# A hybrid decoder trunk on one core: the recurrent branch's gate tiles computed in a fifth product stage

## The chip, the cores and the metric

One core of a Trainium2 chip runs the whole program. The metric is the device time in microseconds (us) of one execution. TensorE (PE) multiplies, VectorE (DVE), ScalarE (ACT) and GpSimd (POOL) work elementwise, SyncE (SP) only issues transfers. Each engine takes its instructions in the order of the program and waits for the others through semaphores. A transfer is issued by SP or POOL, in that queue's own order too.

## The reference

One layer over 1024 tokens of width 1024, all float32. The normalised, modulated input `h` goes through one projection, whose column groups feed two branches; the branches are gated, merged and projected back.

```python
h = rms_norm(x, norm_w[l]) * (1.0 + scale[:, None, :]) + shift[:, None, :]
proj = h @ w_in[l]
hq, hf, hi, hz, gq, gk, gv, gz, ga, mg = jnp.split(proj, IN_OFFSETS, axis=-1)
y_h = hgrn2_branch(hq, hf, hi, hz, lb_all[l], hgrn_norm_w[l])     # ... return rms_norm(o, norm_w) * silu(hz)
y_g = gla_branch(gq, gk, gv, gz, ga, ...)                         # ... return rms_norm(o, norm_w) * silu(gz)
u_h = y_h @ w_branch[l, 0]
u_g = y_g @ w_branch[l, 1]
mg = jax.nn.sigmoid(mg.reshape(B, T, N_BRANCH, D_MODEL))
merged = mg[:, :, 0] * u_h + mg[:, :, 1] * u_g
x = x + gate[:, None, :] * (merged @ w_out[l])
return rms_norm(x, final_norm_w)
```

Both branches are chunked linear attention with a decay for each key channel (8 heads of 128 in the recurrent branch `hgrn2`, 4 heads in `gla`). The change is about `silu(hz)`: 1024 columns of the projection, the gate of the recurrent branch.

## The kernel before

Every float32 matrix product is done as three fp32r products: each operand is split into a rounded part `hi` (a cast on ACT) and a rest `lo = x - hi` (a subtraction on DVE), and `hi*hi + hi*lo + lo*hi` is accumulated. All large tiles are slots of 128 x 1024 float32; there are 46 (`N_SLOTS`), handed out first in, first out, so a slot that was just freed is taken last.

The program has three parts.

**The stream** (`Stream.go`). A list of jobs runs one after the other on PE. A `Feat` job computes 128 columns of the projection for all 1024 tokens: 8 steps of 6 matmuls 128x512 (L455). For each recurrent head there are three, for `hq`, `hf` and `hz`. `Vblk` and `Vblk2` (L514 to L516, L557 to L559) do the values. Each job's weights are loaded up to two jobs ahead and split one job ahead. After each step of 6 matmuls `weave` lets two other tracks put in work: the side track (`attention` of the heads that are ready, faster by the factor `PACE`) and the back track (`prepare`, then `gate_side`, which makes the residual gate from eight blocks of `ada_w`, and the factors of the `gla` branch).

**The stages** (`last_stages`). Four products of 1024 x 1024 x 1024 follow: the two halves of `mg`, and the two branch projections. Each is done by seven products of half-size blocks instead of eight, by sums and differences of blocks. Stage `b` has the groups (b, p) for the seven products `p` in `PRODUCTS`; a group has four pairs `i` of output tiles, each pair 12 matmuls 128x512 (L1293). So a stage has 7 x 4 x 12 = 336 of them. Product p needs one combination of weight blocks and one of activation blocks:

- weight combinations are made on the back track by `weight_sums`: two loads on SP's queue (L1163), four additions on DVE (L1169 to L1173), four stores on POOL's queue (L1175). In a stage `load_duo` loads them on SP (L1222, L1226), and `prep_duo` splits them (ACT L1233, DVE L1234).
- activation combinations are made by `factors` (loads L1126, differences L1138, stores L1139) from the blocks of `h`, of `yg` and of `yh`; for `yh` each block is first multiplied by the branch's norm `mul` (L1132). `fetch_factor` loads one on SP (L1202) and `build` splits it (ACT L1214 and L1211, DVE L1215 and L1212). Stage 1 uses the split factors of stage 0 again (`H[0 if self.b == 1 else self.b, p]`), so nothing is fetched or built for it.

A product is accumulated in a PSUM bank of 128x512 floats. After a group, `Pair.after` copies banks out as snapshots (L1269, L1271), puts a snapshot into another bank (L1276), or adds a bank to a snapshot (L1280). The banks are kept by `Banks`: four from the tiles `pd`, and two from the score tile `sc_ps`, lent once all attention heads have their scores. The first stage's sigmoid gate is stored to DRAM (L1367) and loaded again as `gate` in stage 1 (L1377). Stage order: `mg` half 1, `mg` half 0, branch `gla`, branch `hgrn2`.

**The output** (`OutBlk`, L1076 to L1078): 384 matmuls, the residual and the last norm.

Before the stream there is a start of about 130 us. The build puts the instructions of each engine into an order of its own, near the order of the code, by due times that it works out; what stands on each engine is read from the built program.

## Time and profile before

| | us |
|---|---|
| median of 3 runs (lowest to highest) | 1280.7 (1278.77 to 1281.05) |
| profiled execution, its own time | 1281.29 |
| its span, first to last instruction | 1279.6 |
| DMA moved | 195.05 MB, mean 152 GB/s |

How to read it: the span is what the profiler saw between the first and the last instruction, and lies 1.7 us under that execution's time. Rows of groups give the line, the engine, the operation, `out<-in` with buffer numbers left out, the shape and the count, then the busy time in us and the mean ns of one; behind the second bar stands the idle time of the engine just before them and what ended most of it. `b` is any slot. A window's row gives for each engine the busy us in that stretch, with the number of instructions in brackets.

### The profile page before, as it was taken

Reading aid. Unit: us, or ns where it says so; the run is one execution under the profiler, and the core shown is the slowest. Engines: PE = TensorE matmul, PEld = TensorE weight load, DVE = VectorE, ACT = ScalarE, POOL = GpSimd, SP = SyncE. Lnnn points to the kernel's source line nnn. Section 1 sums busy time; section 2 is a strip of 40 time slices with the busy share of each in tenths; the row PEclk is TensorE's granted clock in tenths of the full one; section 3 lists DMA queues with packets and bytes.
Section 4 is the critical chain, followed back from the end, with each engine's and each line's share of the span. In section 5 each row is a group of like instructions: output and inputs, shape, how many; then the busy total and the mean of one; then the engine's idle time right before and its main releaser. Section 6 shows DMA issues by size and latency. Waiting matters only on the chain. (4 is left out here: it accounts for less than half of the span.)

```text
span 1279.6 us, 20905 instructions
## 1 busy us (share of the span) xinstructions
PE 1219.5 (95%) x8603; PEld 1002.3 (78%) x8603; DVE 802.6 (63%) x1239; ACT 506.3 (40%) x754; POOL 151.4 (12%) x246
## 2 busy tenths in 40 slices
PE   4899999999999999999999999999998999998997
PEld 3677899879797877787787878877786777776885
DVE  5746334785849475876874576686544555659643
ACT  4466612333333223323322233356544454364222
POOL 5510000101111121121220101011121000000000
PEclk9799999999999999999999999999999999999999
DMA  8733100654553266363272511336579846445402
GB/s 270 274 104 93 40 18 18 230 165 129 186 155 134 83 191 221 100 198 126 99 264 100 180 39 62 101 123 208 171 254 335 279 168 204 164 133 178 167 34 99
DMA packets 134129, 195.05 MB, mean 152 GB/s; under 512 B 7819, under 2 KB 97985, under 8 KB 134034
## 3 DMA queue, kind: packets, MB, share of 16 engines
q1 hardware_dynamic: 118114, 140.01, 34.9%
q0 software_dynamic: 15872, 53.70, 10.9%
q8 instruction: 67, 1.10, 0.3%
q14 instruction: 28, 0.23, 0.1%
q10 hardware_dynamic: 48, 0.01, 0.0%
HBM read 140.21 MB, written 53.48 MB: 151 GB/s over the span
## 5 line engine op out<-in xcount | busy, mean ns | idle before, releaser
L455 PE MATMUL pd<-b,b 128*128 128x512 f32 x1632 | 396.9, 397 | 0.0
L455 PEld LDWEIGHTS pd<-b,b 128*128 128x128 f32 x1632 | 301.1, 189 | 64.1 <-issue 1.2
L1293 PE MATMUL pd<-b,b 128*128 128x512 f32 x912 | 221.7, 395 | 12.6 <-ACT pd L1276 5.3
L1293 PEld LDWEIGHTS pd<-b,b 128*128 128x128 f32 x912 | 170.0, 189 | 55.0 <-ACT pd L1276 6.5
L196 DVE TENSOR_TENSOR b<-b,b 128x1024 fp32r<-128x1024 f32 (+1 forms) x95 | 101.0, 1072 | 69.4 <-ACT b L193 41.7
L193 ACT CAST b<-b 128x1024 fp32r<-128x1024 f32 (+1 forms) x95 | 84.6, 905 | 140.4 <-DMA ws<-b 16.8
L1293 PE MATMUL sc_ps<-b,b 128*128 128x512 f32 x432 | 108.6, 397 | 3.9 <-DVE b L1280 2.1
L1293 PEld LDWEIGHTS sc_ps<-b,b 128*128 128x128 f32 x432 | 81.2, 190 | 24.0 <-DVE b L1280 2.5
L1234 DVE TENSOR_TENSOR b<-b,b 128x1024 fp32r<-128x1024 f32 x56 | 68.0, 1222 | 45.3 <-ACT b L1233 28.6
L1233 ACT CAST b<-b 128x1024 fp32r<-128x1024 f32 x56 | 58.2, 1049 | 50.0 <-PE pd L1293 14.1
L514 PE MATMUL pd<-b,b 128*128 128x256 f32 x256 | 75.6, 295 | 0.0
L516 PE MATMUL pd<-b,b 128*128 128x256 f32 x256 | 72.5, 283 | 0.0
L515 PE MATMUL pd<-b,b 128*128 128x256 f32 x256 | 72.5, 283 | 0.0
L1175 POOL DMA_DIRECT2D ws<-b x64 | 35.3, 552 | 205.3 <-DVE b L1169 82.2
L1215 DVE TENSOR_TENSOR b<-b,b 128x1024 fp32r<-128x1024 f32 x36 | 43.4, 1220 | 25.5 <-ACT b L1214 14.1
L557 PE MATMUL pd<-b,b 128*128 128x512 f32 x128 | 51.9, 405 | 0.0
L1214 ACT CAST b<-b 128x1024 fp32r<-128x1024 f32 x36 | 37.6, 1050 | 35.2 <-PE pd L1293 10.0
L559 PE MATMUL pd<-b,b 128*128 128x512 f32 x128 | 50.2, 392 | 0.0
L558 PE MATMUL pd<-b,b 128*128 128x512 f32 x128 | 50.0, 390 | 0.0
L514 PEld LDWEIGHTS pd<-b,b 128*128 128x128 f32 x256 | 49.0, 191 | 0.5
L515 PEld LDWEIGHTS pd<-b,b 128*128 128x128 f32 x256 | 48.9, 191 | 0.6
L516 PEld LDWEIGHTS pd<-b,b 128*128 128x128 f32 x256 | 48.9, 191 | 0.0
(249 smaller groups left out, 1964.9 us busy)
## 6 DMA issues: line engine op xcount, KB each, us to landing
b<-in_w_in_dram SPq DMA_DIRECT2D x66, 512.0 KB, 4.0
ws<-b POOLq DMA_DIRECT2D x64, 256.0 KB, 3.1
b<-ws SPq DMA_DIRECT2D x32, 512.0 KB, 4.9
b<-in_x_dram SPq DMA_DIRECT2D x16, 512.0 KB, 6.7
b<-in_ada_w_dram SPq DMA_DIRECT2D x32, 256.0 KB, 6.0
b<-in_w_branch_dram SPq DMA_DIRECT2D x16, 512.0 KB, 4.8
b<-h SPq DMA_DIRECT2D x14, 512.0 KB, 4.3
b<-yg SPq DMA_DIRECT2D x14, 512.0 KB, 4.4
```

What stands on the lines that cost most here:

```text
L193: i = nc.scalar.copy(hi, src)
L196: (eng or nc.vector).tensor_sub(lo, src, hi.bitcast(F32))
L455: nc.tensor.matmul(ps[0:w, th * 512:(th + 1) * 512], a[:, k, 0:w], b[:, th * 512:(th + 1) * 512], start=(k == 0 and n == 0), stop=(k == KT ...
L514: nc.tensor.matmul(o, lh, hi[:, k % 4, :], start=(k == 0), stop=False)
L515: nc.tensor.matmul(o, lh, lo[:, k % 4, :], start=False, stop=False)
L516: nc.tensor.matmul(o, ll, hi[:, k % 4, :], start=False, stop=(k == KT - 1))
L557: nc.tensor.matmul(o, lh, hi[:, k % 2, :], start=(k == 0), stop=False)
L558: nc.tensor.matmul(o, lh, lo[:, k % 2, :], start=False, stop=False)
L559: nc.tensor.matmul(o, ll, hi[:, k % 2, :], start=False, stop=(k == KT - 1))
L1233: nc.scalar.copy(hi, t)
L1234: nc.vector.tensor_sub(lo, t, hi.bitcast(F32))
L1293: nc.tensor.matmul(o, a[:, sl], c, start=(p in (1, 5) and kt == 0 and n == 0), stop=(kt == 3 and n == 2), skip_group_check=True)
```

## The change

The eight `Feat` jobs of `hz` leave the stream. Their 1024 columns become stage 0 of now five stages, in seven products like the others. Its outputs, `silu` of the gate, stay on chip (`gate_z`, eight slots). The heads' outputs are therefore stored without the gate, and a new `gated_factors` multiplies the blocks of `yh` by the gate and by the norm before it makes the branch's factors. The factors of `h` are fetched and built anew for the stages 1 and 2; in stage 0 the products 1, 2 and 3 take the split `h` of the stream as it stands (`factor`, `drop`). The sigmoid gates stay on chip instead of going through DRAM. The banks are four instead of six, and product 3 comes before 6, so that its bank can be used on. The loads of `weight_sums` and of `factors` go from SP's queue to POOL's, `weight_sums` works in place, and its stores write four pieces of 128 floats in each partition row instead of one of 512. The `gla` gate uses one `Silu` on ACT instead of a sigmoid and a product.

```diff
-PACE = 1.1
-PRODUCTS = (1, 2, 5, 6, 3, 7, 4)
+PACE = 1.15
+PRODUCTS = (1, 2, 5, 3, 6, 7, 4)
 SUMS = {5: 0, 6: 1, 3: 2, 7: 3}
-SEEDS = {(6, 2): 0, (6, 3): 1, (3, 0): 2, (3, 1): 3}
...
+    def gz_done(key):
+        def f(ps):
+            s = g_state[key] = S.get([T])
+            nc.scalar.activation(s, ps, AF.Silu)
...
-            nc.vector.scalar_tensor_tensor(y[0][:, sl], po, vec[:, R_HN + h:R_HN + h + 1],
-                                           y[0][:, sl], ALU.mult, ALU.mult)
+            nc.scalar.activation(y[0][:, sl], po, AF.Copy, scale=vec[:, R_HN + h:R_HN + h + 1])
...
-        J.append(Feat(col(C_HZ + h * P), rhs_h, silu_done(h_state, ("z", h))))
...
+    def load_blocks(acts, names, kk, queue):
+        y = {}
+        for b in names:
+            y[b] = S.get([T])
+            queue.dma_start(y[b], part_of(acts, int(b[0]) - 1, int(b[1]) - 1, kk))
+        return y
...
+    def gated_factors(acts, gates, f, mul):
+        for kk in range(2):
+            y = {}
+            for names in (("12", "11"), ("22", "21")):
+                while len(S.free_list) < 10:
+                    yield 1
+                y.update(load_blocks(acts, names, kk, nc.gpsimd))
+                yield 6
+                for b in names:
+                    half = int(b[1]) - 1
+                    z = gates.pop((half, (int(b[0]) - 1) * 2 + kk))
+                    v = y[b].rearrange("p (a t) -> p a t", a=2)
+                    nc.vector.tensor_mul(v, v, z)
+                    S.free(z)
+                    yield 2
+                    nc.vector.tensor_mul(v, v, mul[:, half * 512:half * 512 + 512].unsqueeze(1).to_broadcast([P, 2, 512]))
+                    if b != "12":
+                        nc.gpsimd.dma_start(f[{"11": 1, "22": 3, "21": 2}[b]][kk], y[b])
+                    yield 2
+            yield 4
+            yield from differences(y, f, kk)
+        S.free(mul)
...
-    sources = [[col(C_MG + n * D + d * P, 2 * P) for d in range(0, 8, 2)] for n in (1, 0)]
+    sources = [[col(c0 + d * P, 2 * P) for d in range(0, 8, 2)] for c0 in (C_HZ, C_MG + D, C_MG)]
...
     def weight_sums(b, i):
         src = sources[b][i]
-        while len(S.free_list) < 12:
+        while len(S.free_list) < 9:
             yield 1
         x1, x2 = S.get([4, 2, P]), S.get([4, 2, P])
         for kh, x in enumerate((x1, x2)):
-            nc.sync.dma_start(x.rearrange("p k a f -> p k (a f)"),
-                              src[kh * 512:(kh + 1) * 512, :].rearrange("(k p) f -> p k f", p=P))
+            nc.gpsimd.dma_start(x.rearrange("p k a f -> p k (a f)"),
+                                src[kh * 512:(kh + 1) * 512, :].rearrange("(k p) f -> p k f", p=P))
         yield 6
...
-    GROUPS = [(b, p) for b in range(4) for p in PRODUCTS]
-    BUILT = [g for g in GROUPS if g[0] != 1]
+    GROUPS = [(b, p) for b in range(5) for p in PRODUCTS]
+    BUILT = [g for g in GROUPS if g not in ((0, 1), (0, 2), (0, 3))]
...
-    f_of = [f_x, f_x, f_g, f_h]
+    f_of = [f_x, f_x, f_x, f_g, f_h]
...
+    def factor(b, p, kt):
+        if (b, p) in H:
+            return (z[kt // 2][:, kt % 2, :] for z in H[b, p])
+        k, half = {1: (kt, 0), 2: (4 + kt, 0), 3: (4 + kt, 1)}[p]
+        return (z[k][:, half * 512:half * 512 + 512] for z in (h_hi, h_lo))
...
             elif p == 5:
                 snap[5] = self.snap_of("e")
-                R.free(bank.pop("e"))
-                self.seed("b", snap[1])
-                Q.free(snap.pop(1))
-            elif p == 6:
-                snap[6] = self.snap_of("b", -1.0)
             elif p == 3:
-                self.summed(0, 1, None, bank["e"], ALU.subtract, 6)
-                R.free(bank.pop("e"))
+                snap[3] = self.snap_of("e")
+                bank["b"] = bank.pop("e")
+                t = snap.pop(1)
+                nc.scalar.copy(bank["b"], t)
+                Q.free(t)
+            elif p == 6:
+                self.summed(0, 1, "b", 3, -1.0)
             elif p == 7:
-                self.summed(1, 1, bank["b"], None, ALU.add, 5)
+                self.summed(1, 1, "b", 5)
...
-    outs[:] = [put_gate1, put_gate0, put_t1, put_m]
+    outs[:] = [put_z, put_gate(gate1), put_gate(gate0), put_t1, put_m]
...
-    after(0, 2, 3, scores_done)
-    after(1, 2, 3, lambda: stream.back.append([factors(yh_d, f_h, rst_h[0]), 1]))
+    after(1, 2, 3, lambda: stream.back.append([gated_factors(yh_d, gate_z, f_h, rst_h[0]), 1]))
```

The built program has 6787 matmul instructions on PE before and 6739 with the change, 48 fewer. What is moved on the other engines shows at three places.

First, POOL's queue in the middle of the stream, before: only stores of weight sums (L1175) and of the branch `gla` (`yg`, L816).

```order
L1175 DMA ws_812<-b_3000 128x512
L1175 DMA ws_809<-b_2999 128x512
L1175 DMA ws_810<-b_2999 128x512
L1175 DMA ws_811<-b_3000 128x512
L1175 DMA ws_816<-b_3186 128x512
L1175 DMA ws_813<-b_3185 128x512
```

The same place with the change (L1183 loads, L1193 stores of weight sums, L885 the sum of squares of a `gla` head).

```order
L1183 DMA b_3619<-in_w_in_dram 128x4x256
L1183 DMA b_3620<-in_w_in_dram 128x4x256
L1193 DMA ws_824<-b_3619 128x4x128
L1193 DMA ws_821<-b_3619 128x4x128
L1193 DMA ws_822<-b_3620 128x4x128
L1193 DMA ws_823<-b_3620 128x4x128
L1183 DMA b_4006<-in_w_in_dram 128x4x256
L1193 DMA ws_824<-b_4006 128x4x128
L1183 DMA b_4126<-in_w_in_dram 128x4x256
L1183 DMA b_4007<-in_w_in_dram 128x4x256
L885 TENSOR_TENSOR b_3859<-b_3859,b_3901 128x1024
```

Loads now stand between stores, and a store waits for DVE's additions before the load behind it can be issued.

Second, DVE around `gate_side` (L953, L955: the eight products with `ada_w`). Before, they stand in the stream, among a head's attention (L677 to L737), the split of a `Feat` (L196) and its gate (L853).

```order
L953 TENSOR_SCALAR b_6466<-b_6469,cs 128x1024
L196 TENSOR_TENSOR b_6479<-b_6354,b_6478 128x1024
L677 TENSOR_TENSOR b_5643<-b_5643,tot_775 128x16x32
L678 TENSOR_TENSOR b_5822<-b_5822,tot_775 128x16x32
L196 TENSOR_TENSOR b_6567<-b_6445,b_6566 128x1024
L677 TENSOR_TENSOR b_5643<-b_5643,tot_775 128x8x64
```

With the change they stand in stage 0, among the attention of the last head and the stage's own splits (L1231 is `build`, L1266 `prep_duo`, L1290 `summed`).

```order
L955 SCALAR_TENSOR_TENSOR b_7190<-b_7362,cs,b_7190 128x1024
L641 COPY_PREDICATED blk<-mask_750,sc_ps 128x8x4
L638 COPY_PREDICATED blk<-mask_750,sc_ps 128x8x4
L639 COPY_PREDICATED blk<-mask_750,sc_ps 128x8x8
L955 SCALAR_TENSOR_TENSOR b_7190<-b_7371,cs,b_7190 128x1024
L640 COPY_PREDICATED blk<-mask_750,sc_ps 128x8x8
L1290 SCALAR_TENSOR_TENSOR b_7173<-pd_6686,b_7173 128x512
L641 COPY_PREDICATED blk<-mask_750,sc_ps 128x8x4
L1231 TENSOR_TENSOR b_7379<-b_7281,b_7377 128x1024
L1231 TENSOR_TENSOR b_7380<-b_7282,b_7378 128x1024
L1266 TENSOR_TENSOR b_7401<-b_7211,b_7400 128x1024
```

The attention of the last two heads, `gate_side` and half of the `gla` factors now lie in stage 0; before, only the last head's attention did.

Third, SP's queue in the stage of the second `mg` half. Before (stage 1) it loads weight combinations (L1222, L1226) and the stored gate.

```order
L1222 DMA b_8501<-ws_820 128x1024
L1377 DMA b_8619<-gate_3_844 128x1024
L1222 DMA b_8538<-ws_824 128x1024
L1377 DMA b_8555<-gate_0_841 128x1024
L1377 DMA b_8574<-gate_1_842 128x1024
L1377 DMA b_8668<-gate_5_846 128x1024
```

With the change (stage 2; here L1222 is `fetch_factor`, L1254 and L1258 are `load_duo`) it loads a pair of factors for each product.

```order
L1254 DMA b_8607<-ws_830 128x1024
L1254 DMA b_8567<-ws_826 128x1024
L1222 DMA b_8585<-fx_781 128x1024
L1222 DMA b_8586<-fx_782 128x1024
L1258 DMA b_8825<-in_w_branch_dram 128x4x128 x2
L1258 DMA b_8780<-in_w_in_dram 128x4x128
L1222 DMA b_8669<-fx_783 128x1024
L1254 DMA b_8652<-ws_828 128x1024
L1222 DMA b_8670<-fx_784 128x1024
```

Eight gate loads are gone there, and two loads of factors stand before each product.

221 lines of the change are left out of this document (89 added, 132 removed).

## The prediction

> **What bounds the kernel now.** I read the page first, then the windows by stage, then the chain of waits and the groups by line. The page's first part and the first row below it settle the engine.
>
> ```profile
> span 1279.6 us, 20905 instructions
> PE 1219.5 (95%) x8603; PEld 1002.3 (78%) x8603; DVE 802.6 (63%) x1239; ACT 506.3 (40%) x754; POOL 151.4 (12%) x246
> ```
>
> PE is busy 95% of the span. Where the other 60 us lie shows in windows cut at the stages (the stream, the four stages, the output; columns are the stretch and its length, then PE, PEld, DVE, ACT and POOL busy, granted clock, DMA share and GB/s).
>
> ```profile
> 128.80:837.70 708.90, 698.49 (x6135) 589.70 (x6134) 469.38 (x795) 232.72 (x342) 87.41 (x120) 1.00 0.40 129
> 837.70:931.40 93.70, 90.55 (x632) 71.83 (x631) 60.58 (x80) 53.42 (x79) 11.91 (x18) 1.00 0.52 166
> 931.40:1019.30 87.90, 81.17 (x337) 64.79 (x337) 45.39 (x42) 38.47 (x55) 12.26 (x23) 0.96 0.85 292
> 1019.30:1100.50 81.20, 78.05 (x337) 62.45 (x336) 48.11 (x52) 41.21 (x50) 0.00 (x0) 1.00 0.58 193
> 1100.50:1183.10 82.60, 78.05 (x339) 62.66 (x338) 58.31 (x74) 42.51 (x58) 0.00 (x0) 1.00 0.48 156
> ```
>
> The stream leaves PE idle for 10.4 of 708.9 us, the stages for 3.2, 6.7, 3.2 and 4.6. What a stage would take without any wait comes from the chain of waits, in an undisturbed place (start, length, what):
>
> ```profile
> 1050.33 2.73 PE pd L1293 x12
> ...
> 1056.74 3.02 PE pd L1293 x12
> ```
>
> Twelve matmuls in a run take 2.73 us, 0.2275 each; after a wait, 3.02. A stage of 336 needs 336 x 0.2275 = 76.4 us. So the stages 1, 2 and 3, which hold almost nothing else on PE, lose 87.9 - 76.4 = 11.5, 4.8 and 6.2 us; that is about 1.5 times their idle time, since PE also starts slowly again. Stage 0 has a head's matmuls between; 1.5 x 3.2 gives about 5. Sum of the four: 27.5. The largest, stage 1, is told by the same chain:
>
> ```profile
> 979.84 8.28 DMA b<-yh
> ...
> 991.58 5.26 DMA fh<-b
> ...
> 996.93 1.24 DVE b L1138
> ```
>
> A load of `yh` takes 8.3 us while the DMA is 85% busy in that stage; DVE stands at the product that needs it, and the splits behind it come late for PE.
>
> **The change, part by part.** The eight `hz` jobs are 8 x 48 = 384 matmuls, the new stage has 336. All are 128x512, so PE's own work falls by 48 x 0.2275 = **-10.9 us**. The heads' own matmuls only move from the stream into stage 0. This much is certain: PE is the bound, and the work is on it.
>
> The price is on what feeds PE. The rows by line:
>
> ```profile
> L1234 DVE TENSOR_TENSOR b<-b,b 128x1024 fp32r<-128x1024 f32 x56 | 68.0, 1222 | 45.3 <-ACT b L1233 28.6 <-DMA gate<-b 5.1 <-issue 2.7
> L1215 DVE TENSOR_TENSOR b<-b,b 128x1024 fp32r<-128x1024 f32 x36 | 43.4, 1220 | 25.5 <-ACT b L1214 14.1 <-PE pd L1293 5.2 <-issue 3.3
> L1233 ACT CAST b<-b 128x1024 fp32r<-128x1024 f32 x56 | 58.2, 1049 | 50.0 <-PE pd L1293 14.1 <-PE sc_ps L1293 11.9 <-DMA b<-in_w_branch_dram 6.6
> L853 DVE TENSOR_TENSOR b<-b,pd 128x1024 f32<-128x1024 f32 x24 | 29.4, 1223 | 11.9 <-ACT b L852 11.8
> L997 DVE SCALAR_TENSOR_TENSOR b<-pm,vec,b 128x512 f32<-128x512 f32 x16 | 12.0, 748 | 6.3 <-ACT b L996 6.2
> L1170 DVE TENSOR_TENSOR b<-b,b 128x512 f32<-128x512 f32 x16 | 11.0, 690 | 13.7 <-DMA b<-in_w_branch_dram 8.7 <-PE pm L709 2.2 <-PE pm L750 1.8
> L955 DVE SCALAR_TENSOR_TENSOR b<-b,cs,b 128x1024 f32<-128x1024 f32 x7 | 10.5, 1494 | 4.9 <-DMA b<-in_ada_w_dram 4.8
> L1138 DVE TENSOR_TENSOR b<-b,b 128x1024 f32<-128x1024 f32 x24 | 30.7, 1290 | 4.7 <-DMA fh<-b 3.5 <-DMA b<-h 1.0
> L1017 DVE RECIPROCAL b<-b 128x256 f32<-128x256 f32 x4 | 6.6, 1708 | 0.8 <-ACT b L865 0.8
> L590 DVE TENSOR_TENSOR xb<-b,b 128x256 f32<-128x256 f32 x12 | 7.8, 647 | 0.0
> L737 DVE SCALAR_TENSOR_TENSOR b<-b,tot,pm 128x128 f32<-128x128 f32 (+1 forms) x72 | 28.1, 390 | 23.3 <-PE pm L731 22.1
> ```
>
> Builds go from 21 to 32 products: 22 casts and 22 subtractions more. Fourteen weight duos, 16 additions for sums, 8 adds of snapshots and 8 gate products come on top; 8 `Feat` splits, 16 gate products (L853) and 16 scalings (L997) go, the last to ACT. On DVE that is 22 x 1.22 + 14 x 1.22 + 16 x 0.69 + 8 x 0.69 + 8 x 1.22 - 8 x 1.22 - 16 x 1.22 - 16 x 0.75 = +29 us; on ACT, with casts at 1.05, about +40 us. Over a span with DVE at 63% and ACT at 40% this hides. It does not hide evenly.
>
> *Stage 0* is where it gathers. The order puts there 14 weight subtractions (17 us), 11 factor subtractions (13), the 8 products of `gate_side` (12), 4 reciprocals (7), 4 differences (5), 8 sums (6), and one and a half to two heads. The 31 rows of `attention` on DVE (L590 the first, L737 the last) sum to 272 us for 12 heads, 22.7 a head: 34 to 45. Together 94 to 105 us, in a stage that has 101 us of PE's work: the old stage 0's 93.7 less 76.4 less 5 leave 12.3 for its one head, and now it is two. The same sum for the old stage 0 gives 64 where the window shows 60.6, so I take 95. How full can DVE get without stopping PE? In windows of 100 us of the stream the fullest are
>
> ```profile
> 229.00:329.00 100.00, 97.85 (x862) 86.02 (x861) 78.27 (x116) 33.05 (x46) 16.23 (x24) 1.00 0.58 193
> 529.00:629.00 100.00, 97.23 (x970) 79.77 (x969) 75.80 (x137) 31.88 (x51) 18.68 (x25) 0.98 0.42 135
> ```
>
> 78%, with 2 to 3 us of PE idle. At 78%, 95 us of DVE take 122: 20 us of loss. Below, stage 0 loses 5 as now. I take 12, the middle, since 94% lies beyond every row.
>
> *Stages 1 and 2.* Stage 1 had no factors to fetch; now it and stage 2 load 2 x 512 KB for each of 14 groups, some 95 GB/s. The gate's way through DRAM goes (16 x 256 KB stored, and loaded again), and the pass over `yh` waits more between its loads (76 units of 6 matmuls instead of 48), so it runs on into stage 2. I keep 11.5 for stage 1 (bounds 4.8, a quiet stage, and 15) and take 6 for stage 2 (4.8 to 11.5). Stages 3 and 4 are the old 2 and 3: 4.8 and 6.2. The four banks instead of six are freed by rows such as these, and the gate's DRAM way is the third.
>
> ```profile
> L1271 ACT ACTIVATE b<-pd 128x512 f32<-128x512 f32 x23 | 13.6, 594 | 15.5 <-PE pd L1293 15.4
> L1280 DVE TENSOR_TENSOR b<-pd,b 128x512 f32<-128x512 f32 x11 | 7.5, 686 | 1.4 <-PE pd L1293 1.3
> ...
> gate<-b POOLq DMA_DIRECT2D x16, 256.0 KB, 2.7
> ```
>
> A bank is wanted again three pairs later, 3 x 2.73 = 8.2 us, and is freed by one operation of 0.6 to 0.7 us, so the loss of two costs nothing while DVE is less than 8 us late; where it is later, PE stands anyway for its splits. Sum of the five: 12 + 11.5 + 6 + 4.8 + 6.2 = 40.5, against 27.5: **+13 us**.
>
> *The stream.* SP's queue gets free of loads of sums that waited for slots, the longest for 25 us; POOL's gets them between stores that wait for DVE.
>
> ```profile
> L1163 SPq EVENT_SEMAPHORE  x38: 17/22/25031, 270.1 to 582.2; - x38
> ...
>   DVE b L1170: 8.7, 3
> ...
> b<-in_w_in_dram SPq DMA_DIRECT2D x66, 512.0 KB, 4.0
> b<-yg SPq DMA_DIRECT2D x14, 512.0 KB, 4.4
> b<-yh POOLq DMA_DIRECT2D x8, 512.0 KB, 7.2
> ```
>
> DVE waited 8.7 us for such loads. Queued behind a waiting addition on DVE are the attention and the splits, so PE follows. I counted in both orders the loads that have less than 6 us of matmul work between the point from which they can be issued and the point from which a late result stops PE: in the stream 14 of 211 before, 30 of 190 now; in the stages 24 of 155 and 41 of 201. With landings of 4.0 to 7.2 us those are the ones that can stop PE. Bounds: -2, if the stream's 10.4 us of idle only shrink with its length and SP runs ahead; +10, if they double with that count. I take +3, nearer to the lower end, since an addition of a sum is not itself waited for until the stages.
>
> The Trainium skill ("DMA: Bandwidth & Descriptors", Issuing engines are not separate DMA queues) speaks against a gain here: transfers from all queues run on the same 16 DMA engines, and another queue saves only the sequencer's time. The trace does not contradict it: 7.2 us on POOL's queue fall in the stage at 85% DMA, 4.4 on SP's in stages at half of that. The same page's Specifications put the first byte at about 1 us from GpSimd and 0.6 from SP; 40 loads with 0.4 us more, all on the path, would be 16 us by an estimate from that page, instead of my +3, and the sum +18 instead of +5.
>
> Sum: -10.9 + 13 + 3 = **+5 us** on the span of 1279.6, 1284.7. The profiled execution took 1281.3, 0.6 over the median; against the median of 1280.7 I predict **1286**.
>
> **The rivals.**
>
> *The gain comes through* (not slower). For it: the removed work is on the engine that is busy 95%; stage 2 shows that a stage with fetches loses only 4.8; the gate's DRAM traffic, which helps to fill the DMA in stage 1, is gone. Against it: DVE's 95 us in stage 0. Then stage 0 loses 8, stage 1 falls to 6, the others 4.8, 4.8 and 6.2, 29.8 in all, and the stream gives -2: -10.9 + 2.3 - 2 = -10.6, **1270**. It decides from the point where DVE in stage 0 can run over 90% busy.
>
> *DVE becomes the bound and `yh` still fills the DMA.* Stage 0 loses 20, stages 1 and 2 lose 11.5 each, the stream +8: -10.9 + (20 + 11.5 + 11.5 + 4.8 + 6.2 - 27.5) + 8 = +24, **1304**. For it: 8.3 us for one load of `yh`, and loads and stores in turn on one queue. Against it: the pass over `yh` is spread wider.
>
> *Nothing to be measured*: losses grow by just what PE saves, within 0.2% of 1280.7 (2.6 us, about what a measurement of this kernel can tell from no change), 1278 to 1283.
>
> **How the numbers follow.** The forecast (1283 to 1296) 0.37; the gain 0.33; DVE and DMA 0.20; nothing 0.10. So faster 0.33, same 0.10, slower 0.57. Since both signs hold much of the chance, the range spans them: down to 1268, below which no row allows more than the saved matmuls and a little of the stages' loss, up to 1307, a little over the second rival. The forecast's own range is 1283 to 1296.
>
> **What would show it.** 48 x 7 x 5 = 1680 matmuls in the stages, 1248 in `Feat` jobs. Stage 0 of about 113 us with DVE over 80% busy, PE waiting there for the subtractions of `prep_duo` and `build`; stage 1 near 88, stage 2 near 82, 3 and 4 as the old 2 and 3. DVE waiting more than 9 us in the stream for loads of sums. I am wrong if stage 0 ends within 107 us, or if the stream takes less than 708.9 less the moved work (87.4 of `Feat` and one head's 12.3), about 609 us.

## The result, and the profile after

The changed kernel takes **1346.1 us** (median of 4 runs, 1336.3 to 1353.2) against 1280.9 for the kernel before in the same job: a ratio of 1.049, 95% interval 1.041 to 1.058. It is slower, by 65 us; the prediction said 1286 and at most 1307. The profiled execution took 1349.1 us, 3.0 over the median; 1.7 us of that time lie outside its span. (Of the runs below, a2 was profiled in an execution of 2408.8 us, where its other four took 1320.1 to 1329.3, so no lengths of stages are given for it.) The page of the changed kernel, first part:

```profile
span 1347.4 us, 20955 instructions
PE 1238.5 (92%) x8555; PEld 1004.0 (75%) x8555; DVE 822.9 (61%) x1267; ACT 546.5 (41%) x807; POOL 203.5 (15%) x302
```

PE has 48 matmuls less to do and is busy 19 us longer than before (1219.5). The windows by stage, cut as for the kernel before (stream, stages 0 to 4, output; stretch and length, then PE, PEld, DVE, ACT, POOL busy, granted clock, DMA share, GB/s):

```profile
127.80:775.90 648.10, 609.53 (x5452) 515.12 (x5451) 398.42 (x709) 206.72 (x311) 139.45 (x180) 0.97 0.41 128
775.90:896.60 120.70, 109.77 (x931) 84.80 (x930) 90.58 (x138) 70.60 (x107) 12.54 (x16) 0.96 0.64 213
896.60:988.40 91.80, 82.51 (x337) 64.28 (x337) 55.93 (x52) 45.34 (x60) 7.49 (x14) 0.96 0.68 224
988.40:1079.10 90.70, 81.77 (x337) 64.06 (x336) 50.92 (x48) 46.02 (x61) 4.27 (x8) 0.96 0.63 214
1079.10:1162.70 83.60, 78.78 (x338) 62.03 (x337) 47.64 (x51) 37.32 (x46) 0.00 (x0) 1.00 0.55 176
1162.70:1252.20 89.50, 86.12 (x359) 66.92 (x358) 62.10 (x79) 43.41 (x56) 0.00 (x0) 0.98 0.48 160
1252.20:1347.40 95.20, 83.99 (x363) 67.14 (x361) 42.42 (x71) 25.53 (x54) 0.00 (x0) 0.97 0.22 82
```

Length less PE's busy time is what PE stood idle. From the stream on that is 38.6 + 10.9 + 9.3 + 8.9 + 4.8 + 3.4 + 11.2 = 87.1 us; in the kernel before, with its last window (output, 96.7 us, 9.0 idle), 37.0. PE's busy time in the same windows is 1132.5 us, before 1113.6. So the span's 67.8 us more are 50.1 us of idle time and 18.9 us of busy time, with 1.2 us less ahead of the stream. The work fell by 10.9, so matmuls that ran slowly cost 18.9 + 10.9 = 29.8 us: 0.6 us for each microsecond of new idle time. The stream alone has 28.2 us of the new idle time, though it lost just the matmuls that the order showed (6135 to 5452).

The longest stall lies at 683 us. The chain of waits there (start, length, what):

```profile
675.91 15.03 DMA b<-in_w_in_dram
...
694.40 1.51 PE sc_ps L625 x64
```

and the timelines of SP's queue and of ACT (last in brackets: idle time before, and what ended it):

```profile
654.24 22.65 SPq L435 DMA_DIRECT2D b<-in_w_in_dram  x4
```

```profile
691.04 1.04 ACT L192 CAST b<-b 128x1024 fp32r<-128x1024 f32 x1 [16.08 <-DMA b<-in_w_in_dram]
691.99 0.40 ACT L618 COPY xb<-b 128x256 f32<-128x256 f32 x1
```

A load of a `Feat` job's weights took 15.03 us, where the median of its line is 4.4; ACT stood 16 us at its cast, with two copies of the attention (L618, L619) behind it, on which DVE and then PE's scores wait. The load was late in its issue too. SP had stood 55.4 us at the first of the four loads in that row, until a matmul of the attention (L725) had ended, presumably the last reader of the slot that the load goes to:

```profile
SPq L435 <- PE pm L725: 95.5, 2, 55.4
```

Two of the four could be issued only after a split on DVE (L195) had ended at 675.35 us, and the load of the chain, the last of them, left at 675.9, when ACT had stood for about 1 us. Landed in 4.4 us it would still have kept ACT for some 5 us, by an estimate from these numbers; the other 10 or so are its slow landing. The windows tell what the DMA did meanwhile and what the stall cost afterwards:

```profile
665.00:690.00 25.00, 18.53 (x143) 14.92 (x141) 14.48 (x18) 5.16 (x6) 12.87 (x16) 0.91 0.82 257
690.00:700.00 10.00, 5.60 (x75) 4.70 (x76) 7.05 (x20) 2.81 (x4) 2.79 (x5) 0.53 0.36 109
```

The DMA is 82% busy while several steps of weight sums load and store (the last step's additions start at 696 us, before at 617), and PE goes on at a granted clock of 0.53. That the full DMA made the load slow is the likely reading; no run shows it alone.

### The profile page after: what moved, and what is told of

Read it like the earlier page. It is cut to its first block, busy times and chain, and to the rows that moved or that the text cites. A ratio compares the mean times of both kernels' runs of the same rounds, so it can differ in the third digit from the quotient of the medians.

```text
span 1347.4 us, 20955 instructions
## 1 busy us (share of the span) xinstructions
PE 1238.5 (92%) x8555; PEld 1004.0 (75%) x8555; DVE 822.9 (61%) x1267; ACT 546.5 (41%) x807; POOL 203.5 (15%) x302
## 4 chain that ended last, share of the span: by engine, by line
PE 51%; issue 12%; DMA 11%; DVE 9%; ACT 4%; POOL 2%; SPq 0%; POOLq 0%; DVEq 0%; ACTq 0%
PE pd L1302 19%; PE pd L453 11%; DMA b<-in_w_in_dram 4%; DMA b<-fx 2%; PE pm L742 2%; PE pd L1074 2%; PE pd L512 2%; PE pd L514 2%; PE pm L725 2%; PE pd L513 2%; PE pd L1076 1%; PE pd L1075 1%; PE pm L744 1%; DVE b L195 1%; DMA b<-in_w_branch_dram 1%
## 5 line engine op out<-in xcount | busy, mean ns | idle before, releaser
L1302 PE MATMUL pd<-b,b 128*128 128x512 f32 x1680 | 412.9, 403 | 28.7 <-ACT b L1280 8.7
L1302 PEld LDWEIGHTS pd<-b,b 128*128 128x128 f32 x1680 | 316.9, 193 | 115.7 <-ACT pd L1323 12.1
L453 PE MATMUL pd<-b,b 128*128 128x512 f32 x1248 | 313.7, 405 | 0.0
L453 PEld LDWEIGHTS pd<-b,b 128*128 128x128 f32 x1248 | 235.0, 193 | 50.4 <-issue 0.5
L1231 DVE TENSOR_TENSOR b<-b,b 128x1024 fp32r<-128x1024 f32 x64 | 79.6, 1255 | 84.7 <-ACT b L1230 68.7
L195 DVE TENSOR_TENSOR b<-b,b 128x1024 fp32r<-128x1024 f32 (+1 forms) x87 | 95.2, 1104 | 57.6 <-PE pd L514 26.4
L192 ACT CAST b<-b 128x1024 fp32r<-128x1024 f32 (+1 forms) x87 | 76.3, 891 | 118.2 <-DMA b<-in_w_in_dram 33.2
L1266 DVE TENSOR_TENSOR b<-b,b 128x1024 fp32r<-128x1024 f32 x70 | 85.2, 1221 | 39.3 <-ACT b L1265 28.1
L1265 ACT CAST b<-b 128x1024 fp32r<-128x1024 f32 x70 | 73.5, 1051 | 75.9 <-PE pd L1302 37.6
L1230 ACT CAST b<-b 128x1024 fp32r<-128x1024 f32 x64 | 66.9, 1049 | 67.5 <-PE pd L1302 28.0
L1193 POOL DMA_DIRECT2D ws<-b x80 | 60.1, 754 | 135.4 <-DVE b L1187 52.8
L512 PE MATMUL pd<-b,b 128*128 128x256 f32 x256 | 75.2, 294 | 0.0
L555 PE MATMUL pd<-b,b 128*128 128x512 f32 x128 | 52.7, 412 | 0.0
L742 PE MATMUL pm<-scT,b 128*128 128x128 f32 x256 | 47.6, 278 | 4.4 <-DVE b L731 4.4
L556 PE MATMUL pd<-b,b 128*128 128x512 f32 x128 | 50.4, 394 | 0.0
L557 PE MATMUL pd<-b,b 128*128 128x512 f32 x128 | 50.2, 393 | 0.0
L512 PEld LDWEIGHTS pd<-b,b 128*128 128x128 f32 x256 | 49.0, 191 | 0.6
L513 PEld LDWEIGHTS pd<-b,b 128*128 128x128 f32 x256 | 49.0, 191 | 0.5
L514 PEld LDWEIGHTS pd<-b,b 128*128 128x128 f32 x256 | 48.9, 191 | 0.0
L742 PEld LDWEIGHTS pm<-scT,b 128*128 128x128 f32 x256 | 39.5, 193 | 7.2 <-DVE b L731 5.7
```

What stands on the lines that cost most here:

```text
L192: i = nc.scalar.copy(hi, src)
L195: (eng or nc.vector).tensor_sub(lo, src, hi.bitcast(F32))
L453: nc.tensor.matmul(ps[0:w, th * 512:(th + 1) * 512], a[:, k, 0:w], b[:, th * 512:(th + 1) * 512], start=(k == 0 and n == 0), stop=(k == KT ...
L512: nc.tensor.matmul(o, lh, hi[:, k % 4, :], start=(k == 0), stop=False)
L513: nc.tensor.matmul(o, lh, lo[:, k % 4, :], start=False, stop=False)
L514: nc.tensor.matmul(o, ll, hi[:, k % 4, :], start=False, stop=(k == KT - 1))
```

## The experiments

All times are medians of 4 or 5 runs, b1's of 10; the kernel before took 1279.3 to 1280.7 us beside each of them. Lengths of stages are from windows like those above, "idle" is PE's idle time from the stream on, worked out as above.

| kernel | us | ratio to before, 95% interval | stream | stage 0 | 1 | 2 | idle |
|---|---|---|---|---|---|---|---|
| before | 1280.7 | | 708.9 | 93.7 | 87.9 | 81.2 | 37.0 |
| the change | 1346.1 | 1.049 (1.041 to 1.058) | 648.1 | 120.7 | 91.8 | 90.7 | 87.1 |
| a1 | 1329.6 | 1.038 (1.033 to 1.043) | 633.7 | 118.8 | 86.9 | 88.9 | 74.7 |
| a2 | 1324.9 | 1.033 (1.028 to 1.038) | | | | | |
| a3 | 1329.8 | 1.037 (1.033 to 1.041) | 632.7 | 119.1 | 89.4 | 90.8 | 74.9 |
| b1 | 1285.2 | 1.003 (1.001 to 1.005) | 712.5 | 93.4 | 88.1 | 81.4 | 40.0 |
| b2 | 1288.1 | 1.006 (1.004 to 1.008) | 718.2 | 94.0 | 89.3 | 81.2 | 41.3 |
| c1 | 1320.1 | 1.029 (1.026 to 1.033) | 618.4 | 117.9 | 93.8 | 91.4 | 67.9 |
| c3 | 1339.3 | 1.046 (1.042 to 1.051) | 644.5 | 118.7 | 86.2 | 88.2 | 82.4 |
| c4 | 1344.5 | 1.048 (1.044 to 1.052) | 642.3 | 115.4 | 93.8 | 90.7 | 86.0 |
| d1 | 1329.9 | 1.037 (1.033 to 1.042) | 636.6 | 111.2 | 87.0 | 91.2 | 71.7 |
| e1 | 1332.9 | 1.041 (1.038 to 1.044) | 632.7 | 120.7 | 87.1 | 90.6 | 75.2 |
| e2 | 1338.6 | 1.046 (1.044 to 1.049) | 640.2 | 121.3 | 90.1 | 87.1 | 78.8 |
| e4 | 1330.9 | 1.041 (1.038 to 1.044) | 635.5 | 110.0 | 89.9 | 92.4 | 72.8 |
| f1 | 1316.7 | 1.029 (1.023 to 1.034) | 609.1 | 113.8 | 106.3 | 95.8 | 70.4 |
| f2 | 1318.1 | 1.029 (1.025 to 1.034) | 615.1 | 110.1 | 100.3 | 92.5 | 65.8 |
| f4 | 1338.1 | 1.044 (1.038 to 1.050) | 641.2 | 119.8 | 90.2 | 90.7 | 81.1 |
| f5 | 1331.0 | 1.041 (1.035 to 1.047) | 643.0 | 110.1 | 87.6 | 90.0 | 70.1 |
| g1 | 1328.1 | 1.038 (1.035 to 1.041) | 635.0 | 114.4 | 90.6 | 96.1 | 75.2 |
| h1 | 1328.2 | 1.038 (1.033 to 1.042) | 642.8 | 123.2 | 85.4 | 80.0 | 74.2 |

Each length is from one execution. c3, c4, e2, f4 and h1 have the same matmuls in the same order in the stream as the change, and their streams took 640.2 to 644.5 us against its 648.1; stage 2 took 88.9 to 92.4 us in the kernels whose edits leave it as it is. So a difference of a few us in one window is not read as an effect. In the run times, the intervals of c3, c4, e2 and f4 lie for the most part within the change's own, so their gains aren't shown by them; and the single edits that gain 13 to 21 us can't be told from one another. With PACE 1.1 (c1, f1, f2) the stream holds 51 matmuls less than the change's, with 1.2 (f5, g1) 64 more, and the stages hold the difference: these lengths aren't of the same work.

### The queue, the pace and the form of the sums

**a1**, the change with one edit:

```diff
-            nc.gpsimd.dma_start(x.rearrange("p k a f -> p k (a f)"),
+            nc.sync.dma_start(x.rearrange("p k a f -> p k (a f)"),
```

> The changed kernel (1346 us, its stream 648 us) with one edit: the loads of the weight sums go back to SP's queue. Theory Q (the loads on POOL's queue stand behind stores that wait for DVE, land late, and DVE with all that is queued behind it stands): DVE's waits for these loads fall from 48.8 us to about 10, the stream to 612 to 622 us, the run to 1308 to 1322 us. Theory S (slots: gates kept on chip and the lower thresholds leave few free slots, so loads of Feat jobs are issued late, whichever queue the sums use): the stream stays at 638 us or more, the run at 1335 us or more. Theory D (DVE is too full in stage 0 and the stages lose most): stage 0 stays at 120 us by either; what D adds is that the run does not fall below 1330.

1329.6 us. The stream came down by 14 us, not by 26 or more, and the reason of theory Q fell: DVE still waits for these loads, 41 us in all. Theory S had the stream at 638 us or more; at 633.7 it is under that too. The groups of DVE's additions in the change and in a1 (busy, mean ns, idle time before them and what ended it):

```profile
L1187 DVE TENSOR_TENSOR b<-b 128x512 f32<-128x512 f32 x20 | 14.4, 720 | 25.3 <-DMA b<-in_w_in_dram 16.8 <-DMA b<-in_w_branch_dram 8.5
L1188 DVE TENSOR_TENSOR b<-b,b 128x512 f32<-128x512 f32 x20 | 13.8, 690 | 23.5 <-DMA b<-in_w_in_dram 11.8 <-DMA b<-in_w_branch_dram 11.7
```

```profile
L1187 DVE TENSOR_TENSOR b<-b 128x512 f32<-128x512 f32 x20 | 14.9, 747 | 23.1 <-DMA b<-in_w_in_dram 13.1 <-DMA b<-in_w_branch_dram 10.0
L1188 DVE TENSOR_TENSOR b<-b,b 128x512 f32<-128x512 f32 x20 | 13.9, 694 | 17.8 <-DMA b<-in_w_branch_dram 11.2 <-DMA b<-in_w_in_dram 6.6
```

**a2**:

```diff
-PACE = 1.15
+PACE = 1.1
```

> The changed kernel with PACE 1.1 as before instead of 1.15, so that the heads' work is handed out 4% slower beside the same matmuls. Theory Q and theory S: within 4 us of 1346 us, since neither hangs on the heads' pace. Theory P (the denser heads fill DVE and ACT in the stream, and PE waits for their results): the stream falls by 10 to 20 us, with as much as a third of a head more in stage 0, and the run falls by 5 to 15 us.

1324.9 us, 21 less, where theory P gave 5 to 15 and Q and S nothing. f5, below, goes the other way with the pace.

**a3** (with `S.free(x1, x2, s1, s2)`, and 11 free slots instead of 9):

```diff
+        s1, s2 = S.get([2, 4, P]), S.get([2, 4, P])
+        parts = {5: s1[:, 0], 6: s1[:, 1], 3: s2[:, 0], 7: s2[:, 1]}
-        nc.vector.tensor_add(x11, x11, x21)
+        nc.vector.tensor_add(parts[7], x11, x21)
...
-        for p, x in ((7, x11), (5, x21), (6, x22), (3, x12)):
+        for p, x in parts.items():
...
```

> The changed kernel with the weight sums formed in two tiles of their own and stored from rows of 2 KB, as before, instead of in place and stored from four pieces of 512 bytes each (two slots more for each step; the step waits for 11 free slots instead of 9). The issue of such a store by POOL took 754 ns, before 552. Theory Q with the store's form as a part of it: 80 stores by 0.2 us are 16 us less on POOL's queue, loads of sums go out earlier, the stream falls by 5 to 12 us. Theory Q without it (the wait for DVE decides, not the issue): within 4 us of 1346 us. Theory S: slower by 3 us or more, since the step takes two slots more.

1329.8 us, the opposite of what theory S gave. Nearest is theory Q with the store's form: the issue of a store took 549 ns again instead of 754, and the stream fell by 15 us, more than the 5 to 12 that it gave. But DVE's idle time at the additions is nearly as long as without the edit, 25.3 + 21.6 us instead of 25.3 + 23.5, only its releasers differ:

```profile
L1189 DVE TENSOR_TENSOR b<-b 128x512 f32<-128x512 f32 x20 | 13.9, 693 | 25.3 <-PE pd L453 7.3 <-DMA b<-in_w_branch_dram 5.3 <-PE pm L744 4.6
L1190 DVE TENSOR_TENSOR b<-b,b 128x512 f32<-128x512 f32 x20 | 13.8, 689 | 21.6 <-DMA b<-in_w_in_dram 12.1 <-PE pd L453 3.6 <-POOL b L1007 2.6
```

So how long DVE stands at the sums doesn't tell what PE loses.

**b1** and **b2** put two parts of the change into the kernel before, one each: the queue of the loads, and the form of a step.

```diff
-            nc.sync.dma_start(x.rearrange("p k a f -> p k (a f)"),
+            nc.gpsimd.dma_start(x.rearrange("p k a f -> p k (a f)"),
```

> The kernel before (1280.7 us, its stream 708.9 us) with one edit: the loads of the weight sums go to POOL's queue. Theory Q: DVE's waits for them rise from 8.9 us to 25 or more, and the run to 1296 to 1312 us (16 steps of sums instead of 20 in a stream that is 9% longer). Theories S, P and D: within 4 us of 1281 us.

```diff
-        while len(S.free_list) < 12:
+        while len(S.free_list) < 9:
...
-        s1, s2 = S.get([2, 4, P]), S.get([2, 4, P])
+        nc.vector.tensor_add(x11, x11, x21)
+        nc.vector.tensor_add(x21, x21, x22)
...
+        for p, x in ((7, x11), (5, x21), (6, x22), (3, x12)):
...
```

> The kernel before (1280.7 us, stream 708.9) with the changed form of a step alone: sums formed in place in the two loaded tiles, stored from four pieces, started at 9 free slots instead of 12; the loads stay on SP's queue, the steps stay 16. Theory F: the second load is issued 5 us or less before its addition (before: 11.6), DVE's waits for it rise from 8.9 us to 25 to 45, and the run to 1287 to 1300 us. Rival (the form is free as long as the stream has its old length and 16 steps; what costs is the denser stream): the run within 3 us of 1281.

+4.7 and +7.5 us. The first lies far below the 15 us or more that theory Q gave, with DVE's waits for these loads at 15.2 us instead of 25 or more. The second is at the low end of theory F's 6 to 19, with these waits up from 8.9 to 23.6 us, a little under the 25 that it gave. In the old stream each part costs little. The queue's 4.7 us also stay under the prediction's upper bound of 10. The same loads landed 4.5 us (median) after their issue on SP's queue and 5.0 on POOL's. The prediction's estimate from the Trainium skill ("DMA: Bandwidth & Descriptors", Specifications), 0.4 us for each load and all on the path, gives 16 us for its 40 loads and 13 for the 32 that b1 moves; the measured 4.7 stay far under it.

### Is it one jam, or several losses?

**c1** joins a1 and a2, with the differences' loads on SP too (a1's line is left out here):

```diff
-PACE = 1.15
+PACE = 1.1
...
-            y = load_blocks(acts, ("12", "11", "22", "21"), kk, nc.gpsimd)
+            y = load_blocks(acts, ("12", "11", "22", "21"), kk, nc.sync)
```

> The changed kernel with the loads of all preparations of the stream (weight sums, differences of factors) on SP's queue and PACE 1.1: both single edits together, which gave -16.5 us (sums on SP, 1329.6) and -21.2 us (PACE, 1324.9). If they remove different losses: -38 us, 1305 to 1312, the stream 610 to 618 us. If each only breaks the same jam (PE stands for 11 us at 683 us, where four steps of sums fill the DMA), the better of the two is all: 1320 to 1328, the stream about 628 us.

1320.1 us: 26 less where the singles sum to 38, so a1's edit adds 5 us to a2's 21 and most of its own 16.5 is shared. The stall before the scores is still there, 6.6 us at 679.

**d1** and **e1** change a step's slots and its spacing alone:

```diff
-        while len(S.free_list) < 9:
+        while len(S.free_list) < 12:
```

> The changed kernel with one number changed: a step of weight sums starts when 12 slots are free, as before, instead of 9. With the loads on SP's queue DVE still waited 41 us for them, so the queue is not what makes them late. Theory T (with 9 free slots a step gets slots that were freed a moment ago, and its loads stand at their issue until the slot's last reader is done): DVE's waits for the sums' loads fall from 48.8 us to 20 or less, the stream from 648 to 626 to 638 us, the run to 1324 to 1336. Rival, theory B (the DMA engines are full where several steps come together, wherever their slots are from): waits of 35 us or more, the stream within 5 us of 648.

```diff
-        yield 6
+        yield 8.5
...
-        yield 1.5
+        yield 1
...
-        yield 2
+        yield 0
```

> The changed kernel with the step of weight sums spaced anew at the same length: its additions come 8.5 units (51 matmuls) after its loads instead of 6, and the next step follows at once, so each load is written 15 matmuls, 3.4 us, earlier against its addition. In the changed kernel the second load of a step was issued 2.9 us (median of 20) before the addition, before 11.6 (of 16); with 12 slots or on SP's queue it stayed at 1.9 to 4.1 us, with sums in tiles of their own it was 12.6. Theory F (in place, a step's two loads always take the slots that the attention freed last, and stand at their issue until its last reader is done; DVE stands, and all behind it): DVE's waits for these loads fall from 48.8 us to 30 or less, the stream by 8 to 16 us, the run to 1330 to 1338. Theory B (the DMA engines, not the issue, decide): waits of 40 us or more, the run within 4 us of 1346.

1329.9 and 1332.9 us, the run times that theories T and F gave, but not by their mechanism: DVE's waits for the loads stay at 47 and 44 us, where 20 and 30 at most were expected. d1 has a second finding, in stage 0:

```profile
765.40:876.60 111.20, 105.89 (x931) 81.91 (x929) 95.29 (x141) 69.68 (x105) 17.22 (x24) 1.00 0.78 268
```

The same 931 matmuls, more work on DVE than in the change (95.3 us instead of 90.6), the DMA fuller (0.78 instead of 0.64), and 9.5 us shorter. DVE is 86% busy there and PE idle for 5.3 us.

d1 also tells what became of theory S, late `Feat` loads for want of slots. ACT's waits for these loads (L192) are 33.2 us in the change, 14.1 in the kernel before, and 6.5 in d1, where a step of sums leaves more slots free. So slots seem to be a part of the lateness. But PE still stands idle for 30.9 us in d1's stream, so late `Feat` loads aren't the whole loss.

**e4** leaves out the fifth stage's four steps of sums:

```diff
-        for b in range(5):
+        for b in range(1, 5):
...
```

> The changed kernel without the four steps of weight sums of the fifth stage (their loads, additions and stores are left out; stage 0 loads the sums of the next stage in their place, so its products are of other weights). If the steps all cost the stream alike, its excess of 39 us over the 609 us that the moved work leaves falls by a fifth, to about 640 us. If the jam at the end of the stream is what they bring (20 steps reach to 701 us, where the last Feat jobs load, and PE stands 11 us at 683): the stream falls to 615 to 628 us and the run to 1312 to 1326. If the steps are hidden: within 4 us of 1346.

1330.9 us, the stream 635.5. The steps are not hidden, and the jam at their end is gone (no stall of the stream after 500 us is over 3 us), but two thirds of the stream's excess over 609 stay.

**f5** goes the other way with the pace:

```diff
-PACE = 1.15
+PACE = 1.2
```

> The changed kernel with PACE 1.2 instead of 1.15, the other way than the run with 1.1, which took 21 us less. Theory P (the denser the heads stand against the matmuls, the more often PE comes to a result that is not there yet): longer by 8 to 25 us, 1354 to 1371, with more stalls in the stream. Rival (1.1 only shifted the heads past one jam of the DMA at 683 us): any shift breaks the jam, also this one, so 1322 to 1340 us, without the 11 us stall.

1331.0 us, 15 less, as the rival said: not longer. The waits of PE (total, times, longest) in the change and in f5:

```profile
PE sc_ps L625 <- DVE tot L628: 13.6, 2, 10.9
```

```profile
PE sc_ps L625 <- DVE tot L628: 1.8, 3, 0.9
```

The 11 us stall is gone. So part of the loss is where the heads happen to meet the sums' transfers at PACE 1.15, and each of a1, d1, e1, e4 and f5 shortens that stall; in c3, c4, e2, f4 and h1, which leave the stream as it is, it comes back with 10.1 to 12.7 us. It isn't the whole: a3 keeps a stall of 10.2 us there and gains 16 us all the same, and the stream of f5 still has 32.7 us of idle time, in smaller pieces. f5 also says that it isn't the density of the heads as such: 1.1 and 1.2 are both shorter than 1.15.

### The stages

**c3**, **c4** and **e2** move work within the stages:

```diff
-        after(*GROUPS[n - 1], 0, lambda g=g: build(g))
+        after(*GROUPS[n - 1], 1, lambda g=g: build(g))
```

> The changed kernel with the casts of the next group's factor (ACT, then DVE's subtraction) written one pair of output blocks later, so that a fetched factor has 8.2 us to land instead of 5.5. Theory L (in stages 1 and 2 the loads of fresh factors land late, ACT stands at their cast, and the snapshots behind it come late for PE): stages 1 and 2 fall from 91.8 and 90.7 us to 85 to 88 each, the run by 6 to 12 us to 1334 to 1340. Theory Y (the pass over yh makes DVE stand in both stages, fetches are on time without it): both stages within 1.5 us, the run within 4 us of 1346.

1339.3 us; stages 1 and 2 fall by 5.6 and 2.5, both within theory L's 85 to 88 but for 0.2 us. It points to theory L, no more: stage 1 takes 86.9 to 93.8 us in kernels whose edits leave it alone, and c3's 86.2 lies just below. The chain of waits of the change shows the loads that it is about:

```profile
920.27 7.95 DMA b<-fx
...
935.96 6.63 DMA b<-fx
...
949.91 7.86 DMA b<-fx
```

Each ends in a cast (L1230), behind which come the snapshot or the subtraction that PE stands for.

```diff
-                stream.back.append([gate_side(), 4])
+                pass
...
+    after(3, 1, 3, lambda: stream.back.append([gate_side(), 4]))
```

> The changed kernel with gate_side (8 products of DVE, 9 to 12 us, and 8 loads) started in stage 3 instead of stage 0. Theory D (DVE with 91 us of work in stage 0 is what stretches it to 120.7 us): stage 0 falls to 106 to 113 us, stage 3 rises by 3 us or less, the run falls to 1333 to 1341 us. Theory H (what PE waits for in stage 0 are the two heads' own chains between ACT, DVE and PE, however full DVE is): stage 0 stays at 117 us or more, and the run within 4 us of 1346.

1344.5 us, neither theory's picture: stage 0 falls by 5.3 us, stage 3 rises by 5.9. What `gate_side` costs moves with it, and that is PE's own work: eight matmuls, 5.4 us in the change (L963 and L964). Stage 0 of c4:

```profile
770.10:885.50 115.40, 103.89 (x924) 81.98 (x922) 81.43 (x130) 67.48 (x104) 12.56 (x16) 0.97 0.56 190
```

```profile
L963 PE MATMUL pm<-b,ones 128*128 128x512 f32 x4 | 3.2, 886 | 3.7 <-DVE blk L640 3.7
```

DVE has 9 us less to do there than in the change, and PE stands idle as long, 11.5 us instead of 10.9. That speaks against theory D and is what theory H said of the waits.

```diff
-                yield 6
+                yield 12
```

> The changed kernel with 12 units instead of 6 between the loads of two blocks of yh and the products that need them. Theory Y (in stage 2 PE stands 6.3 us at one place because DVE, in order, waits for a load of yh): that wait goes, stage 2 falls from 90.7 us to 83 to 87, the run by 3 to 8 us to 1338 to 1343. Rival (DVE is late there for other reasons, or the pass, which runs longer now, moves its wait into stage 3): stage 2 and 3 together within 2 us of 174.3, the run within 3 us of 1346.

1338.6 us. Stage 2 falls by 3.6 us, to 87.1, below all of the 88.9 to 92.4 that it takes where no edit touches it, and stage 3 keeps its length. So the wait for `yh` costs a little; the run time doesn't show it clear of noise.

**f4** gives the stages six banks again:

```diff
+    def lend():
+        assert not stream.side
+        R.extend([sc_ps[:, 0:512], sc_ps[:, 512:1024]])
+
+    after(1, 2, 3, lend)
...
```

> The changed kernel with the two banks of scores lent to the stages from stage 1 on, six accumulators instead of four, as before. The prediction's step (a bank is wanted again three pairs later and freed by one operation of 0.7 us, so four are enough): the run within 4 us of 1346. Rival (with DVE and ACT late in the stages, a bank comes free late and PE waits for it): stages 1 to 4 shorter by 2 to 4 us each, the run by 8 to 14 us.

1338.1 us, 8 less, yet hardly any of it where the rival had it: in the profiled executions stages 1 to 4 change by -1.6, 0, -1.3 and +0.4 us. 7 us are in the stream, which the edit doesn't touch, and 3 in the output. The intervals of the two kernels overlap. Four banks cost the stages 1 to 4 nothing that can be seen.

**h1** leaves the fresh factors of stages 1 and 2 out:

```diff
-    BUILT = [g for g in GROUPS if g not in ((0, 1), (0, 2), (0, 3))]
+    BUILT = [g for g in GROUPS if g not in ((0, 1), (0, 2), (0, 3)) and (g[0] not in (1, 2) or g == (1, 1))]
...
     def factor(b, p, kt):
+        b, p = (1, 1) if b in (1, 2) else (b, p)
...
     def drop(b, p):
+        if b in (1, 2):
+            if (b, p) != (2, 4):
+                return
+            b, p = 1, 1
```

> The changed kernel with one factor, built once, for all 14 groups of stages 1 and 2 (13 of 32 fetches of two blocks of 512 KB, their 26 casts on ACT and 26 subtractions on DVE are left out; the products of these two stages are of the wrong factors). Theory N (factors made anew in each stage are what those stages lose by: ACT stands for a fetched block, the cast, DVE's subtraction and the snapshots behind them come late): stages 1 and 2 fall from 91.8 and 90.7 us to 78 to 84 each, the run by 12 to 25 us, to 1321 to 1334. Theory Y (the pass over yh with its gate products, loads and stores decides, and would also without the builds): both stages within 3 us of their lengths, the run within 5 us of 1346.

1328.2 us. Its windows of stages 1 and 2:

```profile
891.50:976.90 85.40, 79.35 (x338) 61.86 (x337) 45.06 (x42) 32.16 (x46) 9.12 (x17) 1.00 0.61 203
976.90:1056.90 80.00, 78.74 (x337) 61.93 (x336) 30.46 (x29) 35.50 (x49) 2.14 (x4) 1.00 0.36 119
```

Together 17.1 us less than the change's 182.5, and 10 less than the shortest that the two take where no edit touches them (175.8, a1); stage 2 is as quiet as the old stage 2 (81.2). And the wait for `yh` is longer than in the change (22.1 against 14.9 us), though more of the pass lies in stage 1; PE stands idle in stage 2 for 1.3 us only, with 7.6 us of these waits in it:

```profile
L1155 DVE TENSOR_TENSOR b<-b,b 128x1024 f32<-128x1024 f32 x8 | 9.7, 1223 | 22.1 <-DMA b<-yh 22.1
```

So without the factors the pass over `yh` does next to no harm there. How it harms with them shows at one place of the change's chain, ahead of PE's longest stall in stage 2, 6.1 us:

```profile
1002.38 7.90 DMA b<-yh
...
1010.37 1.24 DVE b L1155
...
1012.77 2.36 DVE b L1231 x2
```

The subtractions of a factor (L1231) stand behind the product with `yh` on DVE, and a load of weights of 4.2 us and the cast of it behind these.

### All edits together

**f1** joins the edits (a3's, c1's, c3's and e2's); a step also waits for slots ahead of its own tiles. **f2** is the same with the sums in place and 12 slots. Of f1's edit, the pace and the new wait:

```diff
-PACE = 1.15
+PACE = 1.1
...
+        while len(S.free_list) < 9:
+            yield 0.5
+        s1, s2 = S.get([2, 4, P]), S.get([2, 4, P])
...
```

> The changed kernel with the edits that helped, together: loads of sums and differences on SP's queue, PACE 1.1, sums in tiles of their own (started at 11 free slots), factor casts one pair later, 12 units ahead of the products with yh. Alone they gave -16.5, -21.2, -16.3, -6.8 and -7.5 us. If they remove different losses, the sum of -68 us holds: 1275 to 1285, no slower than the kernel before. If the three edits in the stream share one loss, as the two of c1 did in part (-26 where their sum was -38): the stream 612 to 620 us, stages 1 and 2 86 to 88 us each, the run 1298 to 1310, still slower than before by 17 us or more, and stage 0 is what is left.

> The same, but with the sums in place and started at 12 free slots, so that of the step's form only the threshold goes back. Theory F (in-place loads are late whatever the threshold): 4 to 10 us over the run with tiles of their own, the loads issued 5 us or less before their addition. Rival (with SP's queue and PACE 1.1 the form no longer matters): within 4 us of it.

1316.7 and 1318.1 us: with the other edits in place the form no longer matters, and the sum of -68 is refuted; both also lie above the 1298 to 1310 that a shared loss in the stream would give. f1's stream and first three stages:

```profile
127.20:736.30 609.10, 594.28 (x5401) 504.42 (x5400) 384.23 (x690) 204.67 (x305) 76.99 (x114) 0.99 0.39 124
736.30:850.10 113.80, 105.51 (x941) 84.50 (x939) 89.19 (x143) 64.08 (x100) 16.29 (x22) 0.97 0.74 257
850.10:956.40 106.30, 93.03 (x381) 70.73 (x381) 67.70 (x63) 53.82 (x71) 12.64 (x15) 0.95 0.65 220
956.40:1052.20 95.80, 82.98 (x338) 64.50 (x337) 52.99 (x49) 46.23 (x60) 5.34 (x10) 0.93 0.64 214
```

The stream's idle time is 14.8 us, near the 10.4 of before, so most of it can be undone. But 51 matmuls less lie in it than in the change's, 44 more in stage 1, and stages 0 to 2 have 34.4 us of idle time where the change has 29.1. The stream's 609.1 us are therefore not yet the 609 of the prediction.

**g1**, against f1:

```diff
-PACE = 1.1
+PACE = 1.2
...
-        while len(S.free_list) < 9:
-            yield 0.5
```

> The changed kernel with sums in tiles of their own (started at 11 free slots) and loaded on SP's queue, factor casts one pair later, 12 units ahead of the products with yh, and PACE 1.2. With PACE 1.1 the same edits (f1) brought the stream to 609 us, where the prediction had it without any loss, but stages 1 and 2 rose to 106.3 and 95.8, with 44 matmuls of a head and the end of the preparations in stage 1. If those two stages pay only for work that came late into them: with PACE 1.2 the stream takes 615 to 625 us, stages 0, 1 and 2 take 108 to 112, 85 to 88 and 86 to 89, and the run 1292 to 1304 us, the shortest with a fifth stage, still over the kernel before. If the loss only changes its place: the sum stays, 1313 to 1322.

1328.1 us: 1292 to 1304 was wrong, and the time lies over the 1313 to 1322 of the other case too. Stage 1 has its 337 matmuls again and takes 90.6 us, but the stream, with 115 matmuls more than f1's, is back at 635.0 and has 26.2 us of idle time, and stage 2 stays at 96.1. The loss mostly changes its place, and 11 us come on top. None of the kernels with a fifth stage comes near 1280.

## Why the prediction was wrong, point by point

- **The work, -10.9 us.** It went as counted: the stream and stage 0 hold the matmuls that the order showed. It is 10.9 us against 80 us of new loss.
- **The stream, +3 (bounds -2 to +10): the step that failed.** It took 648.1 us where 609 were left, +39; five kernels with the same order in the stream took 640.2 to 644.5, which is still +31 to +36. The step was to price the stream by the number of loads with little lead, with idle time growing at most as that number does. The number grew 2.1 times, idle time 3.7 times, by 28.2 us. The sign that it named, DVE waiting more than 9 us for loads of sums, came, with 48.8 us, but it was not the price: with the loads back on SP DVE waited 41 us for them (a1), and with the queue changed alone the kernel before lost 4.7 us (b1). Two parts of the change got no price at all: the pace (a2, 21 us; but f5 shows no rule of denser being slower) and the form of the sums (b2, 7.5). Shown in its place: one stall of 10.9 us, behind a `Feat` load that was issued late and took 15 us, is a part of the loss, and five different edits shorten it; edits of queue, pace and form bring the stream's idle time to 14.8 us together (f1), with some of its work moved behind it; and they overlap, so no share can be given to each. How the rest divides stays open, and so does what the thinner stream costs by itself, for no run has it alone.
- **POOL's queue and the full DMA.** The prediction read the 4.4 us of `yg`'s loads on SP as taken in stages with half of the DMA's load. Eight of these 14 loads lie in the stream (644 to 657 us, the DMA 61% busy), four in the stage at 85% itself. b1 compares like with like: 4.5 us on SP, 5.0 on POOL.
- **Stage 0, +7 (12 instead of 5).** The price came from DVE's fullness. The stage took 120.7 us against 101 of work as counted, but 5 of the 20 are no loss: `gate_side`'s eight matmuls stood in the stream before (745 to 748 us), and the count of 101 left them out (the stream's excess is larger by as much). So the loss is about 15, which is near the 12 by luck, for the reason given doesn't hold: DVE was 75% busy, not over 80%; d1 ran the same matmuls and 95.3 us of DVE work in 111.2 us; and with 9 us of DVE's work taken out PE stood idle as long (c4). Fullness doesn't set it; what does wasn't isolated. (The rows of `attention` sum to 282 us, not 272, which changes little.)
- **Stages 1 and 2, 11.5 and 6.** Measured 15.4 and 14.3 over 76.4. Here a reason that the prediction named, fresh factors to fetch, is right and the size was off: without them the two lose 9.0 and 3.6 (h1). Of the 29.7 us, 17 are theirs against the change's own execution, and 10 against the shortest that the two stages take where no edit touches them. `yh` running on into stage 2 counts for less (e2, 3.6). DVE's waits for ACT's casts of factors, 14.1 us for 36 subtractions before, were 68.7 for 64:

```profile
L1231 DVE TENSOR_TENSOR b<-b,b 128x1024 fp32r<-128x1024 f32 x64 | 79.6, 1255 | 84.7 <-ACT b L1230 68.7 <-PE pd L1302 11.4 <-PE pm L744 3.2
```

- **Stages 3 and 4, 4.8 and 6.2.** 7.2, and 13.1, of which 20 matmuls (4.6 us) are the output's, which began earlier and got 1.5 us shorter.
- **Two banks less cost nothing.** Nothing speaks against it in the stages 1 to 4 (f4).
- **A loss is about 1.5 times the idle time.** Right: 50.1 us of idle time came with 29.8 us of slow matmuls, which makes 1.6.
- **The rivals.** The one that came nearest, +24, had DVE as the bound of stage 0, which it wasn't, and gave the stream 8 us. The forecast's sign held, and PE is still the bound; the size lay outside every case, because none gave the stream more than 10 us.

## What to carry to other kernels

Give every part of a change its price, the pace and the form of the preparations as well as the moved operations; here two unpriced ones were worth 7 to 21 us alone. That 100 us of matmuls less in a stretch of 709 took the slack of all that was left in it is a likely reading, and no run isolates it. An engine's total wait at a line says little about what the bounding engine loses there; 41 to 49 us of waiting for the same loads went with 20 to 39 us of PE's idle time (f2, the change). And a price per late load is no upper bound: late loads meet, and stalls are paid again in slow matmuls (0.6 us for each us of idle time here).
